# Where eighteen weight splits of a hybrid-block kernel run: GpSimd or VectorE

## The chip, the cores and the metric

The kernel runs on one NeuronCore of a Trainium2 chip. The metric is the device time of one execution in microseconds (us). The engines are named as in the profile: PE is TensorE (PEld its weight loads), DVE is VectorE, ACT is ScalarE, POOL is GpSimd, SP is SyncE.

## What is computed

The reference is one layer of a streaming encoder on a sequence of 1024 tokens of width 1024, in float32:

```python
def reference(...):
    x = x + token_mixer(rmsnorm(x, g_mix), w_in, gdn_conv, ..., w_sb_up, w_gdn_up, w_mix_out)
    x = x + memory_cross_attention(rmsnorm(x, g_cross), rmsnorm(mem, g_mem), w_cq, w_ckv, w_co)
    x = x + peer(rmsnorm(x, g_peer), w_pq, subkeys, peer_u, peer_v)
    return rmsnorm(x, g_final)
```

`token_mixer` makes one input projection. Of its columns, 1536 feed eight stick-breaking attention heads (`sb_q`, `sb_k`, `sb_v`), 1536 feed a gated DeltaNet through a causal convolution of width 4 (`g_q`, `g_k`, `g_v`), and the others are gates. `peer` scores 16384 single-neuron experts for every token by product keys, takes 8 x 16 of them, and sums `gelu(peer_u[e] . x) * gate * peer_v[e]` over them.

## The kernel before

The sequence is cut into three groups of 256, 384 and 384 tokens (GROUPS), and the loop at L1030 takes each through token mixing, cross attention and routing. The running state of the DeltaNet and the keys and values pass from group to group.

Every weight matrix goes through `proj` (L226). It takes 128 output columns at a time: SP loads the tile `raw` (128 x 1024), `split` (L85) makes two halves of it, and `mm3` (L219) multiplies. A split is two instructions: ACT copies `raw` into `wh` in the shorter type F32R (L77), and then `wl = raw - wh` is one `tensor_tensor` (L89), on VectorE or, where `split` is given `eng=pool`, on GpSimd. `mm3` issues three matmuls for every one of 8 row blocks: `wh` with the input's high part, `wl` with the high part, `wh` with its low part. There are three buffers of `raw` and two each of `wh` and `wl`.

Which engine makes `wl` is set by the argument `share`: with `share` at n, every n-th column tile has it on GpSimd. Four constants give it (L27): SH_G = 3 for the 12 tiles of the DeltaNet columns (L468), SH_S = 6 for the 12 tiles of the attention columns (L523), SH_R and SH_Z = 0 for routing (L688) and gates (L548), which is none. The other calls of `proj` pass no share. That makes 4 + 2 splits on GpSimd in each group, 18 in all. What follows a DeltaNet tile is a convolution: one ACT copy and three VectorE instructions (`gc`, L474 to L476, recorded at L77 and L83).

Three of the eight blocks of 128 tokens (DENSE = 4, 5, 6) are taken through all experts by dense products. `dense_h` (L932) splits a tile of `peer_u` and multiplies it, `weigh` (L959) splits a tile of `peer_v` and adds into six PSUM tiles. The first 36 tiles of `peer_u` are done ahead of the rest, in `dense_ahead` (L942), where one in four has its `wl` on GpSimd (L948).

The other five blocks gather the chosen rows. `fetch` (L791) issues an indirect DMA of 128 rows (512 KB) from GpSimd's queue into one of seven `row` buffers. Rows of `peer_u` are multiplied with the tokens and summed by one VectorE instruction (L809); rows of `peer_v` are added up on TensorE (L838) or, for blocks 3 and 7, on VectorE (L856, recorded at L83). The gathers of blocks 0 and 1 can begin when group 0 is routed, and run beside groups 1 and 2.

The program is traced in the order of the code and then ordered for each engine by a scheduler that works with its own estimates of durations (`schedule_with_timeline_sim=True`, L1133). The order of each engine's queue is fixed before the kernel starts: an instruction that waits holds all behind it on its engine.

Of the kernel before, what the change touches and what calls it, by code (L numbers as in the profile page):

```python
# [23 lines left out]
NMEM = 256  # L24
GROUPS = ((0, 256), (256, 384), (640, 384))
RG = 4
SH_G, SH_R, SH_S, SH_Z = 3, 0, 6, 0  # L27
DENSE = (4, 5, 6)
AHEAD = 36
FIRST = 320  # L30
SPOT = 1
LATER = 1
SUMMED = (3, 7)
ROWS = 7
# [17 lines left out]
def block_kernel(ctx: ExitStack, tc: tile.TileContext, x_t, mem_t, gains, cst, sel, eye, w_in, conv, a_log,  # L52
# [3 lines left out]
    act, vec, pe, pool, sp = nc.scalar, nc.vector, nc.tensor, nc.gpsimd, nc.sync  # L56

    def open_pool(name, bufs=1, space=None, side=None, where=ctx):
        kw = {}
        if space is not None:  # L60
            kw["space"] = space
        if side is not None:
            kw["side"] = side
        return where.enter_context(tc.tile_pool(name=name, bufs=bufs, **kw))
# [14 lines left out]
    def func(o, i, f, **kw):  # L79
        return act.activation(o, i, f, **kw)  # L80
# [4 lines left out]
    def split(hi, lo, src, scale=1.0, eng=vec):  # L85

        copy(hi, src, scale)
        if scale == 1.0:
            eng.tensor_tensor(lo, src, hi, op=OP.subtract)  # L89
        else:  # L90
            stt(lo, src, scale, hi, OP.mult, OP.subtract)
# [20 lines left out]
    def j_tile():  # L112
        return pp.tile([P, 512], F32, name="pj")
# [4 lines left out]
    def mix(a, b, ratio):  # L118

        n = 0.0  # L120
        for _ in b:
            n += ratio
            while n >= 1.0:
                next(a, None)
                n -= 1.0
        for _ in a:
            pass
# [9 lines left out]
    def run(*its):  # L137
        for _ in steps(*its):
            pass
# [79 lines left out]
    def mm3(ps, wh, wl, hi, lo, kt):  # L219
        i = 0  # L220
        for k in range(kt):
            for a, b in ((wh, hi), (wl, hi), (wh, lo)):
                pe.matmul(ps, lhsT=a[:, k], rhs=b[:, k], start=i == 0, stop=i == 3 * kt - 1)  # L223
                i += 1
# [692 lines left out]
    def pick_stored(tmp):  # L917
        for i, blk in enumerate(order):
            if i >= nlast:
                sel3 = tmp.tile([P, 3, P], F32, name="sel3")  # L920
                sp.dma_start(sel3, sel_sc[blk])
                yield from spread(tmp, sel3, i)

    def pick_gates(p2, found, tmp):
        for b in range(nlast):
            sel3 = choose_t(p2, *found(b))
            yield
            yield from spread(tmp, sel3, b)
# [3 lines left out]
    def dense_h(r, xh, xl, ps, o, eng=vec):  # L932

        raw = wp.tile([P, KD, P], F32, name="raw", bufs=3)
        sp.dma_start(raw, ut_v[:, :, r * P:(r + 1) * P])
        uh = wp.tile([P, KD, P], F32R, name="wh")
        ul = wp.tile([P, KD, P], F32R, name="wl", bufs=WLS)
        split(uh, ul, raw, eng=eng)
        mm3(ps, uh, ul, xh, xl, KD)
        func(o, ps, AF.Gelu)  # L940

    def dense_ahead(xh, xl, where):  # L942
        T = ND
        tmp = open_pool("dh", 2, where=where)
        for r0 in range(0, AHEAD, RG):
            h = tmp.tile([P, RG, T], F32, name="h")
            for j in range(RG):
                dense_h(r0 + j, xh, xl, j_tile()[:, :T], h[:, j], pool if j == 3 else vec)  # L948
                yield
            sp.dma_start(h_sc[:, r0:r0 + RG, :T], h)  # L950

# [54 lines left out]
    def retrieve(*blocks):  # L1006
        pending = None
        for blk in blocks:
            keep = []
            its = [retrieve_u(blk, keep)]  # L1010
            if pending:
                its.append(second(*pending))
            yield from steps(*its)
            pending = (blk, keep)
        yield from steps(second(*pending))
# [14 lines left out]
    for g, (t0, T) in enumerate(GROUPS):  # L1030
# [11 lines left out]
        with ex:  # L1042
            if last:
                picked = open_pool("picked", 1, side="right", where=ex)
            cross(g, x1[0], T)
            if last and SPOT == 0:
                run(pick_stored(picked))
# [6 lines left out]
        if g == 1:  # L1054
            run(retrieve(0, 1))
    if SPOT == 1:
        run(pick_stored(picked))
    if not LATER:
        for b in range(nlast, len(late)):
# [6 lines left out]
    with ExitStack() as eh:  # L1066
        mix(pick_gates(pool_c, found, picked), dense_ahead(xh, xl, eh), (nlast * 33) / max(AHEAD, 1))
    if LATER:
        for b in range(nlast, len(late)):
# [67 lines left out]
```

## Time and profile before

| | us |
|---|---|
| median of 3 runs | 3774.82 |
| lowest and highest | 3766.2, 3779.0 |
| the profiled execution, whole | 3750.96 |
| its span, first to last instruction | 3749.2 |
| PE busy in the span | 3356.5 |
| DVE busy | 2831.5 |
| POOL busy | 1848.1 |
| ACT busy | 1646.3 |

The profile is of one execution, and the sums below are made against its 3750.96 us; the median of the runs is 0.6% longer. Busy time of an engine holds the time in which an instruction is stretched by something else. Matmul ends are modelled, so a PE that is busy all the time need not be at its peak; the granted clock (PEclk) tells at which speed it was let run, 1.00 for 2.4 GHz and 0.50 for 1.2 GHz. In the stretches of the span, group 0 reaches to about 560 us, group 1 begins its projections at about 560, group 2 at about 1460, and the dense stage of the experts begins at about 2310, with `weigh` from 2812 on.

### The profile page before, as it was taken

The numbers are of one execution on the slowest core, as the hardware profiler recorded it, in microseconds if no ns is written. First come the engines' busy times: TensorE is split into PE (matmuls) and PEld (weight loads), VectorE is DVE, ScalarE is ACT, GpSimd is POOL, SyncE is SP. The second block draws the span as 40 slices with busy tenths as digits, with TensorE's granted clock in tenths as the row PEclk, the third lists the DMA queues.
The fourth block names the chain that finished last, engine by engine and source line by source line (L and its number), as shares of the span: only waits on it lengthen the run. The fifth ranks groups of instructions, "written<-read, shape, count | busy, mean of one in ns | idle before, by whom it ended". The sixth has DMA issues, their size and how long they took to land. (4 is left out here: it accounts for less than half of the span.)

```text
span 3749.2 us, 56321 instructions
## 1 busy us (share of the span) xinstructions
PE 3356.5 (90%) x20621; PEld 2821.2 (75%) x20621; DVE 2831.5 (76%) x5255; ACT 1646.3 (44%) x3086; POOL 1848.1 (49%) x1419
## 2 busy tenths in 40 slices
PE   7999976899879986999978899999759999999995
PEld 6888866777767774767757677888748999999974
DVE  5445599887566699427896666999887888879886
ACT  5754544654324333545523243367643333333333
POOL 1020006767754555456787545564663555536541
PEclk9999988999989997999969999999979999999998
DMA  5526548997899998999877999999999999989995
GB/s 155 146 85 197 155 127 286 325 314 257 285 361 332 339 343 291 320 312 316 287 251 246 368 302 333 325 338 329 358 366 338 330 340 341 346 294 365 350 381 205
DMA packets 745789, 1100.50 MB, mean 294 GB/s; under 512 B 42148, under 2 KB 554532, under 8 KB 742440
## 3 DMA queue, kind: packets, MB, share of 16 engines
q0 software_dynamic: 184320, 671.17, 49.5%
q1 hardware_dynamic: 561192, 425.73, 36.9%
q8 instruction: 162, 2.65, 0.3%
q14 instruction: 115, 0.94, 0.1%
HBM read 1036.60 MB, written 60.16 MB: 293 GB/s over the span
## 5 line engine op out<-in xcount | busy, mean ns | idle before, releaser
L793 POOL DMA_INDIRECT row<-in_peer_u_dram,ix x640 | 839.0, 1311 | 546.3 <-DVE hh L809 151.6
L809 DVE CUSTOM_DVE_ANT_0 row<-row,xs 128x1024 f32<-128x1024 f32 x640 | 837.9, 1318 | 124.7 <-DMA row<-in_peer_u_dram,ix 110.5
L89 DVE TENSOR_TENSOR wl<-raw,wh 128x1024 fp32r<-128x1024 f32 (+1 forms) x420 | 494.9, 1178 | 278.1 <-ACT wh L77 270.9
L223 PE MATMUL pj<-xhi,wh 128*128 128x384 f32 (+1 forms) x1912 | 640.6, 335 | 56.0 <-ACT xhi L77 21.1
L223 PE MATMUL pj<-xhi,wl 128*128 128x384 f32 (+1 forms) x1912 | 642.3, 336 | 36.6 <-POOL wl L89 24.0
L223 PE MATMUL pj<-xlo,wh 128*128 128x384 f32 (+1 forms) x1912 | 623.5, 329 | 6.2 <-DVE xlo L89 6.2
L793 POOL DMA_INDIRECT row<-in_peer_v_dram,it x384 | 435.6, 1134 | 368.4 <-PE ac L838 163.3
L77 ACT ACTIVATE wh<-raw 128x1024 fp32r<-128x1024 f32 (+1 forms) x447 | 449.9, 1007 | 277.5 <-PE pj L223 193.9
L793 POOL DMA_INDIRECT row<-in_peer_v_dram,ix x256 | 363.3, 1419 | 379.1 <-DVE y L83 200.2
L223 PEld LDWEIGHTS pj<-xhi,wh 128*128 128x128 f32 x1912 | 374.9, 196 | 88.8 <-ACT xhi L77 26.0
L223 PEld LDWEIGHTS pj<-xhi,wl 128*128 128x128 f32 x1912 | 375.3, 196 | 75.4 <-POOL wl L89 26.4
L223 PE MATMUL pj<-xh,wh 128*128 128x384 f32 x1152 | 393.9, 342 | 16.2 <-ACT h L80 12.9
L223 PE MATMUL pj<-xh,wl 128*128 128x384 f32 x1152 | 395.8, 344 | 9.9 <-DVE wl L89 7.5
L223 PE MATMUL pj<-xl,wh 128*128 128x384 f32 x1152 | 391.5, 340 | 0.2 <-DVE xl L89 0.2
L223 PEld LDWEIGHTS pj<-xlo,wh 128*128 128x128 f32 x1912 | 373.3, 196 | 23.6 <-DVE xlo L89 10.1
L83 DVE SCALAR_TENSOR_TENSOR y<-row,hh,y 128x1024 f32<-128x1024 f32 x256 | 330.3, 1290 | 6.0 <-DMA row<-in_peer_v_dram,ix 5.1
L838 PE MATMUL ac<-row,sb 128*32 128x256 f32 x3072 | 264.1, 401 | 37.6 <-DMA row<-in_peer_v_dram,it 35.7
L89 POOL TENSOR_TENSOR wl<-raw,wh 128x1024 fp32r<-128x1024 f32 x27 | 67.0, 2483 | 465.0 <-ACT wh L77 463.6
L223 PEld LDWEIGHTS pj<-xh,wh 128*128 128x128 f32 x1152 | 219.5, 191 | 26.0 <-ACT h L80 13.9
L223 PEld LDWEIGHTS pj<-xh,wl 128*128 128x128 f32 x1152 | 219.4, 190 | 24.2 <-DVE wl L89 9.0
L77 ACT ACTIVATE vh<-vr 128x1024 fp32r<-128x1024 f32 x128 | 135.0, 1058 | 202.5 <-PE pj L974 202.5
L223 PEld LDWEIGHTS pj<-xl,wh 128*128 128x128 f32 x1152 | 219.2, 190 | 1.5 <-DVE xl L89 0.6
(450 smaller groups left out, 6255.2 us busy)
## 6 DMA issues: line engine op xcount, KB each, us to landing
raw<-in_w_in_dram SPq DMA_DIRECT2D x132, 512.0 KB
raw<-in_peer_ut_dram SPq DMA_DIRECT2D x128, 512.0 KB
vr<-in_peer_v_dram SPq DMA_DIRECT2D x128, 512.0 KB
raw<-in_w_pq_dram SPq DMA_DIRECT2D x48, 512.0 KB
g_sc<-st SPq DMA_DIRECT2D x12, 2048.0 KB
gm<-g_sc SPq DMA_DIRECT2D x32, 768.0 KB
raw<-in_w_mix_dram SPq DMA_DIRECT2D x24, 512.0 KB
raw<-in_w_cq_dram SPq DMA_DIRECT2D x24, 512.0 KB
```

The costliest lines, as they stand in the source:

```text
L77: return act.activation(o, i, AF.Copy, scale=scale)
L83: return vec.scalar_tensor_tensor(out=o, in0=a, scalar=s, in1=b, op0=op0, op1=op1)
L89: eng.tensor_tensor(lo, src, hi, op=OP.subtract)
L223: pe.matmul(ps, lhsT=a[:, k], rhs=b[:, k], start=i == 0, stop=i == 3 * kt - 1)
L793: pool.indirect_dma_start(out=t, out_offset=None, in_=src, in_offset=bass.IndirectOffsetOnAxis(ap=index, axis=0))
L809: vec.tensor_tensor_reduce(out=t, in0=t, in1=xs, scale=1.0, scalar=0.0, op0=OP.mult, op1=OP.add, accum_out=hh[:, j:j + 1])
L838: pe.matmul(ac[32 * d:32 * d + 32, 256 * w:256 * w + 256], lhsT=sb[:, j], rhs=t[:, 256 * d:256 * d + 256], start=j == 0, stop=j == 31)
```

## The change

Two constants go to 0, so that `proj` gives no split of the DeltaNet and attention columns to GpSimd any more. The literal 3 in `dense_ahead` becomes a constant of the same value.

```diff
@@ -24,11 +24,12 @@
-SH_G, SH_R, SH_S, SH_Z = 3, 0, 6, 0
+SH_G, SH_R, SH_S, SH_Z = 0, 0, 0, 0
 DENSE = (4, 5, 6)
 AHEAD = 36
 FIRST = 320
 SPOT = 1
+PJ = 3
 LATER = 1
@@ -945,7 +946,7 @@
             for j in range(RG):
-                dense_h(r0 + j, xh, xl, j_tile()[:, :T], h[:, j], pool if j == 3 else vec)
+                dense_h(r0 + j, xh, xl, j_tile()[:, :T], h[:, j], pool if j == PJ else vec)
                 yield
```

## Rows read from the trace of the kernel before

**Rows 1.** The page: busy us by engine; POOL splits with count, busy, mean ns, idle.
```profile
PE 3356.5 (90%) x20621; PEld 2821.2 (75%) x20621; DVE 2831.5 (76%) x5255; ACT 1646.3 (44%) x3086; POOL 1848.1 (49%) x1419
...
L89 POOL TENSOR_TENSOR wl<-raw,wh 128x1024 fp32r<-128x1024 f32 x27 | 67.0, 2483 | 465.0 <-ACT wh L77 463.6
```
**Rows 2.** PE's waits over the span: us in total, times, longest.
```profile
PE ac L838 <- DMA row<-in_peer_v_dram,it: 35.7, 23, 5.1
...
PE pj L223 <- POOL wl L89: 26.3, 10, 10.2
```
**Rows 3.** PE's waits for POOL from 0 to 130, 560 to 750, 1460 to 1650 us.
```profile
PE pj L223 <- POOL wl L89: 2.6, 3, 1.0
...
PE pj L223 <- POOL wl L89: 16.3, 2, 10.2
...
PE pj L223 <- POOL wl L89: 5.2, 1, 5.2
```
**Rows 4.** Timeline, POOL beside DVE: start, us, engine, line, operation, idle before.
```profile
33.17 2.35 POOL L89 TENSOR_TENSOR wl<-raw,wh 128x1024 fp32r<-128x1024 f32 x1 [31.72 <-ACT wh L77]
34.07 2.54 DVE L89 TENSOR_TENSOR wl<-raw,wh 128x1024 fp32r<-128x1024 f32 x1 [4.13 <-ACT wh L77]
...
1525.78 2.38 POOL L89 TENSOR_TENSOR wl<-raw,wh 128x1024 fp32r<-128x1024 f32 x1
1525.97 2.62 DVE L83 SCALAR_TENSOR_TENSOR gc<-ev,cv,gc 128x384 f32<-128x384 f32 x1 [2.56 <-ACT gc L77]
```
**Rows 5.** Durations on DVE over the span: ns shortest, median, longest; first and last start.
```profile
L89 DVE TENSOR_TENSOR wl<-raw,wh x420: 682/1224/3359, 19.1 to 3536.3; 128x1024 fp32r<-128x1024 f32 x124, 128x512 fp32r<-128x512 f32 x16
...
L83 DVE SCALAR_TENSOR_TENSOR gc<-ev,cv,gc x108: 364/610/3391, 36.5 to 1538.6; 128x384 f32<-128x384 f32 x72, 128x256 f32<-128x256 f32 x36
```
**Rows 6.** Timeline in groups 1 and 2: ACT's `wh` and the splits.
```profile
566.19 1.05 ACT L77 ACTIVATE wh<-raw 128x1024 fp32r<-128x1024 f32 x1
570.02 1.22 DVE L89 TENSOR_TENSOR wl<-raw,wh 128x1024 fp32r<-128x1024 f32 x1
580.22 1.05 ACT L77 ACTIVATE wh<-raw 128x1024 fp32r<-128x1024 f32 x1
583.99 1.06 ACT L77 ACTIVATE wh<-raw 128x1024 fp32r<-128x1024 f32 x1 [2.12 <-PE pj L223]
587.62 2.52 POOL L89 TENSOR_TENSOR wl<-raw,wh 128x1024 fp32r<-128x1024 f32 x1
593.96 1.22 DVE L89 TENSOR_TENSOR wl<-raw,wh 128x1024 fp32r<-128x1024 f32 x1
663.51 1.04 ACT L77 ACTIVATE wh<-raw 128x1024 fp32r<-128x1024 f32 x1
667.49 1.21 DVE L89 TENSOR_TENSOR wl<-raw,wh 128x1024 fp32r<-128x1024 f32 x1
672.13 1.04 ACT L77 ACTIVATE wh<-raw 128x1024 fp32r<-128x1024 f32 x1
682.96 2.53 POOL L89 TENSOR_TENSOR wl<-raw,wh 128x1024 fp32r<-128x1024 f32 x1
1463.57 1.05 ACT L77 ACTIVATE wh<-raw 128x1024 fp32r<-128x1024 f32 x1
1465.74 1.22 DVE L89 TENSOR_TENSOR wl<-raw,wh 128x1024 fp32r<-128x1024 f32 x1
1471.17 2.35 POOL L89 TENSOR_TENSOR wl<-raw,wh 128x1024 fp32r<-128x1024 f32 x1
```
**Rows 7.** Windows: stretch, us, busy and count by engine, PEclk, DMA share, GB/s.
```profile
577.00:625.00 48.00, 32.83 (x162) 30.99 (x160) 44.15 (x67) 14.69 (x31) 35.44 (x26) 0.89 0.93 306
...
686.00:690.00 4.00, 4.00 (x14) 4.00 (x14) 4.00 (x8) 0.52 (x1) 3.39 (x3) 0.50 0.90 240
691.00:701.00 10.00, 10.00 (x58) 9.73 (x57) 6.69 (x9) 7.40 (x15) 4.49 (x5) 1.00 1.05 383
...
2830.00:3720.00 890.00, 877.76 (x4345) 785.15 (x4343) 735.81 (x855) 320.04 (x440) 434.39 (x299) 1.00 0.97 335
```

## The prediction

> **What bounds the kernel now.** I read the page first: TensorE (PE) is busy for 3356.5 of 3749.2 us and GpSimd (POOL) for half, and 27 weight splits on POOL take 67.0 us, 2483 ns each [rows 1]. So POOL is not short of time; what counts is who waits for it. The table of waits says that PE idled 26.3 us just in front of matmuls whose `wl` came from POOL, out of some 393 us of idle (3749.2 less 3356.5), and 35.7 us for fetched rows of `peer_v` [rows 2]. Asked by stretch, 2.6 us of the 26.3 lie in the projections of group 0, 16.3 in those of group 1 (two waits, the longer 10.2) and 5.2 in those of group 2, one wait [rows 3]. That is 24.1 us; the remaining 2.2 belong to the splits of L948, which the diff does not touch.
>
> Next I laid the timeline of POOL beside that of VectorE (DVE), and there is a second cost. When a POOL split starts, the two-input DVE instruction that meets it ends only after it: a split of 1.22 us takes 2.54 beside POOL's at 33.17, and a convolution step takes 2.62 beside the one at 1525.78 [rows 4]; the medians of the split and of the convolution step are 1.224 and 0.610 us [rows 5]. The rows given are the first and the last of 16 such meetings among the 18 splits that move; I subtracted the median of the same line, tile and shape from each, which gives 1.27 to 2.78 us each and 31.7 us together.
>
> Last the end of the kernel: from 2830 to 3720 PE is busy 877.76 of 890 us at full clock, with the DMA share at 0.97 [rows 7]. That stage is PE's own work, so an earlier start of it is an earlier end, as long as the row gathers keep up.
>
> **The change part by part.** SH_G and SH_S at 0 move 12 + 6 splits (of every 12 tiles, every third, and every sixth, in three groups) to DVE. PJ = 3 says what the literal said: the 9 splits of L948 stay on POOL.
>
> *DVE's queue.* Added are 18 x 1.224 = 22.0 us [rows 5], gone are the 31.7 us of holding: net 9.7 us less. In group 1, whose DVE is nearly full (44.15 of 48 us busy from 577 to 625 [rows 7]), six meetings cost 13.1 us against 7.3 added: 5.7 us less. I count nothing for this in the forecast and the 5.7 as a possible gain. A rule of the Trainium skill speaks against the change here: "Perfetto Trace Analysis", Optimizing Scalar/DVE Operations, says that where DVE is saturated, moving work to ScalarE or even GpSimd may help; by that alone DVE would be 22.0 us fuller and nothing would come back. The same passage warns that the port the two engines share can spoil such a move, and the 31.7 us of holding in this trace are what it warns of.
>
> *PE's waits, group 0.* ScalarE finishes `wh`, POOL needs about 2.4 us, PE takes `wl` at once. On DVE, mostly idle at those moments, the split is done 1.2 us sooner; the three waits are of at most 1.0 [rows 3]. All 2.6 us go.
>
> *Group 1.* The split at 587.62 had its `wh` at 581.27 (580.22 + 1.05), so it lay 6.35 us in POOL's queue behind fetches, and ended 8.87 after its `wh`; the one at 682.96 had its `wh` at 673.17, lay 9.79 and ended 12.32 after it [rows 6]. How long would DVE keep it? Twelve DVE splits between 566 and 672 show delays of 0.03 to 8.91 us, mean 3.44: the first waits 2.77 (from 567.25 to 570.02), the worst 8.91 (585.05 to 593.96), the last 2.94 [rows 6]. With 3.44 + 1.22 = 4.66 the savings are 8.87 - 4.66 = 4.2 and 12.32 - 4.66 = 7.7: 11.9 of the 16.3 us. The other four splits had no wait behind them worth naming. What is next late is DVE itself, with its row reductions.
>
> *Group 2.* `wh` was there at 1464.62, POOL's split began 6.55 later and ended at 1473.52; DVE did a split at 1465.74 and was free for another at 1466.96 [rows 6]. That ends at 1468.2, before PE has stalled: all 5.2 us go.
>
> *The granted clock.* After the waits PE runs at half speed for a while: from 686 to 690 it is granted 0.50 (1.2 GHz), with 14 matmuls in 4 us, against 58 in 10 us at 1.00 (2.4 GHz) right behind [rows 7]. 14 matmuls at 5.8 per us are 2.4 us of work, so 1.6 us were lost. Three such stretches, about 4.6 us. The waits of group 1 only shrink, so I count the 1.6 of group 2 alone.
>
> *POOL.* It gets 18 x 2.4 = 43 us back, and the fetches behind each split can be issued earlier. Whether one lands earlier depends on free row buffers and the DMA queues: between a loss of nothing and a gain that the rows do not show. I take 0.
>
> Sum: 2.6 + 11.9 + 5.2 + 1.6 = 21.3 us. Of this 18.7 arise in groups 1 and 2, beside the gathers, whose rows come at their own pace. Bounds: none of the 18.7 carries to the end if the gathers set it, all of it if PE does. Being 18.7 us earlier, PE would leave about six more rows to the last stage (POOL's 299 instructions there are fetches, 34 per 100 us); at 0.52 MB each (128 rows of 4 KB) and 335 GB/s [rows 7] that is 10 us of transfer in a stage of 0.97 share, of which some fits. The stage looks like PE's, so I keep three quarters: 2.6 + 14.0 = 16.6 us. The profiled execution took 3750.96 us (span 3749.2, 1.8 around it), 0.6% under the median of the runs, 3774.82. 3750.96 - 16.6 = 3734.4 is a ratio of 0.9956; on the median that is **3758 us**.
>
> **The rivals.**
> 1. *The gathers hold the end.* Only group 0's 2.6 us remain, since the gathers start after it: 3772 us. For: DMA share 0.97 in the last stage, waits for rows [rows 2, 7]. Against: PE hardly waits in that stage.
> 2. *DVE's queue becomes the wait* (slower). The moved splits stand in group 1 behind row reductions that wait for DMA. If all six are served like the worst of the twelve, they end 6 x (8.91 + 1.22) = 60.8 us after their `wh` in sum, against 34.7 now (delays 0.08, 6.35, 2.08, 1.58, 9.79, 0.13 and the splits' own times): 26.1 later, less 9.4 from groups 0 and 2: 16.7 us slower, 3792. It decides from a mean delay of 4.57 us on (POOL's mean 3.34 plus the 1.23 that DVE is quicker). For: DVE is 92% busy there. Against: the mean of its delays is 3.44, and holding goes. The Trainium skill's rule above, without its warning, would end in this rival.
> 3. *More than forecast.* All waits of POOL go (24.1), with the clock (4.6) and DVE's relief (5.7): 34.4 us, 3740.
> 4. *The change doesn't do what it says.* The title speaks of none on GpSimd, while nine splits stay there; they concern 2.2 us of waits, so the time does not hang on it.
>
> Over all lies that the order of every engine's queue is made anew from estimated durations (L1133), so that instructions far from the splits may change places. In the trace a single bad place costs PE 5 to 10 us (5.1 longest for rows, 10.2 for a POOL split [rows 2, 3]); two of them either way are 16 to 20.
>
> **How the numbers follow.** 0.3%, about what a measurement can tell here, is 11 us. Forecast (3758) 0.38, of which 0.04 ends within 0.3%; more (3740) 0.12; gathers (3772) 0.22; DVE's queue (3792) 0.28. Faster 0.34 + 0.12 = 0.46, same 0.04 + 0.22 = 0.26, slower 0.28. The range takes in 3740 and 3792 and a misplacement of 16 to 20 us beyond each: 3720 to 3808. The likeliest case alone spans 3740 to 3772.
>
> **What would show it.** POOL keeps nine instructions of L89 and DVE has 438 of that tile; no PE wait is put down to POOL `wl` before 2400; convolution steps and row reductions beside the old places are back at their medians (those beside the splits of L948 stay long); PE's waits on DVE `wl` grow by less than 24 us. The first two waits in group 1 are down to a few us, and the last stage starts some 15 us earlier. The forecast is wrong if PE's waits on DVE `wl` in 560 to 750 pass 16 us, if the stage from 2830 is longer by what was gained, or if large waits stand at lines that hold no split.

## The result, and the profile after

The changed kernel takes 3754.66 us (median of 13 runs, 3744.07 to 3765.22), the kernel before 3774.82 (13 runs). The ratio is 0.9945, 95% interval 0.9934 to 0.9955: 20 us less, where 3758 was forecast. Put on a chip again, it gave 0.9961 (0.9944 to 0.9977).

The forecast time was close; the place was not. The profile of before that the prediction rests on is of an execution 24 us under its median, so totals of the two first profiles can't be set against each other; a second profile of the kernel before (3773.59 us, below) is used where places are compared. In the changed kernel all lines behind L31 have numbers one higher.

The page of the changed kernel, busy us by engine:
```profile
PE 3363.0 (89%) x20621; PEld 2831.3 (75%) x20621; DVE 2820.2 (75%) x5273; ACT 1650.5 (44%) x3089; POOL 1840.4 (49%) x1401
...
L90 DVE TENSOR_TENSOR wl<-raw,wh 128x1024 fp32r<-128x1024 f32 (+1 forms) x438 | 513.1, 1172 | 260.6 <-ACT wh L78 246.4
```
Eighteen instructions have gone from POOL to DVE, and yet DVE is busy 11 us less than in [rows 1]. The durations on DVE say why (ns shortest, median, longest; first and last start):
```profile
L84 DVE SCALAR_TENSOR_TENSOR gc<-ev,cv,gc x108: 364/605/682, 34.8 to 1539.5; 128x384 f32<-128x384 f32 x72, 128x256 f32<-128x256 f32 x36
```
The longest convolution step was 3.391 us in [rows 5] and is 0.682 now. The timeline of VectorE in group 0, where a tile is 256 columns wide. The kernel before (first profile) has six convolution steps of 4.86 us in sum beside the POOL split at 47.27, and three of 3.32 beside the one at 58.57:
```profile
46.66 4.86 DVE L83 SCALAR_TENSOR_TENSOR gc<-ev,cv,gc 128x256 f32<-128x256 f32 x6
...
58.96 3.32 DVE L83 SCALAR_TENSOR_TENSOR gc<-ev,cv,gc 128x256 f32<-128x256 f32 x3 [0.91 <-ACT gc L77]
```
The changed kernel, in its second run, whose file keeps the old line numbers:
```profile
48.05 1.23 DVE L89 TENSOR_TENSOR wl<-raw,wh 128x1024 fp32r<-128x1024 f32 x1 [0.16 <-ACT wh L77]
49.19 1.52 DVE L83 SCALAR_TENSOR_TENSOR gc<-ev,cv,gc 128x256 f32<-128x256 f32 x3
50.88 1.23 DVE L89 TENSOR_TENSOR wl<-raw,wh 128x1024 fp32r<-128x1024 f32 x1 [0.17 <-ACT wh L77]
52.02 1.52 DVE L83 SCALAR_TENSOR_TENSOR gc<-ev,cv,gc 128x256 f32<-128x256 f32 x3
53.72 1.22 DVE L89 TENSOR_TENSOR wl<-raw,wh 128x1024 fp32r<-128x1024 f32 x1 [0.18 <-ACT wh L77]
```
A tile comes every 2.83 us, one split and three convolution steps, with hardly a gap. The 19 us from 45 to 64 by window (us, then busy time and count of PE, PEld, DVE, ACT and POOL, then granted clock, DMA share and GB/s); first the kernel before, from its first profile:
```profile
45.00:64.00 19.00, 15.63 (x122) 14.75 (x123) 15.84 (x20) 10.66 (x28) 5.04 (x2) 1.00 0.50 139
```
and the changed kernel, from its own first:
```profile
45.00:64.00 19.00, 19.00 (x163) 19.00 (x162) 17.60 (x29) 12.78 (x35) 0.00 (x0) 1.00 0.69 167
```
PE ran 163 matmuls instead of 122, at the same granted clock.

To see where a lead is made and lost, I read off each trace when ACT begins the `wh` copy of certain weight tiles (the weight tiles are loaded in one order in all kernels), and when the first fetch starts. First column in us, the others as differences from it:

| | before, second profile | before, first profile | changed, second run | changed, first run | group 0 alone | group 1 alone | group 2 alone | shifted in 1 and 2 | group 0 and shifted |
|---|---|---|---|---|---|---|---|---|---|
| last DeltaNet tile, group 0 | 68.0 | -0.8 | -9.9 | -9.7 | -9.0 | -0.5 | -2.2 | +0.1 | -9.8 |
| last attention tile, group 0 | 110.5 | -0.7 | -13.6 | -13.3 | -12.7 | -0.2 | -2.0 | +0.3 | -13.4 |
| first fetch | 578.6 | -1.8 | -15.8 | -18.8 | -20.0 | -1.4 | -6.1 | -0.4 | -19.6 |
| last attention tile, group 1 | 714.5 | -2.3 | -5.8 | -15.1 | -25.0 | +5.5 | -6.6 | -7.6 | -23.9 |
| first tile, group 2 | 1390.4 | -10.3 | -4.5 | -1.3 | -24.0 | +16.3 | -7.0 | -8.7 | -32.1 |
| last attention tile, group 2 | 1631.4 | -13.7 | -19.3 | -18.5 | -26.0 | +13.2 | -20.0 | -22.7 | -33.6 |
| first dense tile | 2421.1 | -17.5 | -18.0 | -19.3 | -30.2 | +9.7 | -8.8 | -11.4 | -14.6 |
| 37th dense tile | 2704.3 | -21.6 | -15.5 | -15.0 | -27.5 | +1.6 | +2.6 | -11.9 | +6.4 |
| end of the span | 3771.8 | -22.6 | -13.0 | -11.8 | -17.4 | +23.5 | +3.0 | -4.7 | +18.8 |

Each column is one execution. Up to the first fetch the two executions of one kernel lie at most 3.0 us apart; behind it the two of the kernel before drift 10.3 us apart by the first tile of group 2 and 22.6 by the end, with no change of program. A difference behind the first fetch, of one column, is therefore not shown to be the kernel's own unless it is clearly larger.

The lead of the changed kernel is there before the first gather starts. In both of its runs little of it is left at the first tile of group 2, and it is 18 to 19 us at the first dense tile, against the second profile; against the first profile of the kernel before it would be 0.5 to 1.8 there. Only the medians of the runs tell what reaches the end.

### The profile page after: what moved, and what is told of

It is laid out like the page before. It is cut to its first block, busy times and chain, and to the rows that moved or that the text cites. A ratio compares the mean times of both kernels' runs of the same rounds, so it can differ in the third digit from the quotient of the medians.

```text
span 3760.0 us, 56279 instructions
## 1 busy us (share of the span) xinstructions
PE 3363.0 (89%) x20621; PEld 2831.3 (75%) x20621; DVE 2820.2 (75%) x5273; ACT 1650.5 (44%) x3089; POOL 1840.4 (49%) x1401
## 5 line engine op out<-in xcount | busy, mean ns | idle before, releaser
L794 POOL DMA_INDIRECT row<-in_peer_u_dram,ix x640 | 861.3, 1346 | 927.9 <-DMA ix<-id_sc 346.0
L810 DVE CUSTOM_DVE_ANT_0 row<-row,xs 128x1024 f32<-128x1024 f32 x640 | 826.6, 1300 | 130.6 <-DMA row<-in_peer_u_dram,ix 110.4
L90 DVE TENSOR_TENSOR wl<-raw,wh 128x1024 fp32r<-128x1024 f32 (+1 forms) x438 | 513.1, 1172 | 260.6 <-ACT wh L78 246.4
L794 POOL DMA_INDIRECT row<-in_peer_v_dram,ix x256 | 372.3, 1454 | 352.9 <-DVE y L84 171.3
L224 PE MATMUL pj<-xh,wh 128*128 128x384 f32 x1152 | 396.0, 344 | 16.4 <-ACT h L81 13.2
L224 PEld LDWEIGHTS pj<-xh,wh 128*128 128x128 f32 x1152 | 220.4, 191 | 28.3 <-ACT h L81 14.6
L81 ACT ACTIVATE h<-pj 128x384 f32<-128x384 f32 x128 | 62.8, 490 | 327.5 <-PE pj L224 309.5
```

Of the source, the lines that this page charges most:

```text
L794: pool.indirect_dma_start(out=t, out_offset=None, in_=src, in_offset=bass.IndirectOffsetOnAxis(ap=index, axis=0))
L810: vec.tensor_tensor_reduce(out=t, in0=t, in1=xs, scale=1.0, scalar=0.0, op0=OP.mult, op1=OP.add, accum_out=hh[:, j:j + 1])
```

## The experiments

**The kernel before and the changed kernel again, and the change in halves.** The halves make the share depend on the group:
```diff
-            for i, ps in proj(w_in, O_G, 1536, xh, xl, T, share=SH_G):
+            for i, ps in proj(w_in, O_G, 1536, xh, xl, T, share=SH_G if g in (1, 2) else 0):
-                for i, ps in proj(w_in, O_SB, 1536, xh, xl, T, share=SH_S):
+                for i, ps in proj(w_in, O_SB, 1536, xh, xl, T, share=SH_S if g in (1, 2) else 0):
```
for group 0 alone, and `g in (0,)` for groups 1 and 2.

> The kernel before once more, for a second profile: the first one was of an execution 24 us under the median. Up to the first gather (576.8 us) all theories expect the same times within 1 us, behind it differences of up to 20 us with no change of program.

> The changed kernel once more, on the same chip as the two halves. All theories: ratio 0.9934 to 0.9955. If the two halves add, their differences sum to this one. Its profile tells which stretches keep the lead of 16 to 17 us that the first profile shows at the first gather.

> The splits of group 0 alone move to VectorE (6 of the 18); groups 1 and 2 keep theirs on GpSimd. Theory A (the gain is made in group 0, where the splits on GpSimd also hold VectorE's own instructions and so delay every following tile, and it carries to the end): 16 to 20 us less than the kernel before, ratio about 0.995, first gather some 16 us earlier than 576.8. Theory B (the prediction's own sum: most of the gain lies in groups 1 and 2): 2.6 us less, ratio 0.9993. Theory C (the gain comes from queues laid out anew far from the splits): nothing fixed; a first gather that is earlier, with a total that is not.

> The splits of groups 1 and 2 move (12 of 18), those of group 0 stay on GpSimd. Theory A: no change, ratio within 0.998 to 1.002, since in group 1 VectorE's queue keeps a split as long as GpSimd's did. Theory B: 14 us less (three quarters of 18.7), ratio 0.9963. Theory C: nothing fixed.

Measured: group 0 alone 3756.24 us, ratio 0.9962 (0.9950 to 0.9974), 17 us less; groups 1 and 2 together 3779.4, ratio 1.0017 (1.0004 to 1.0030), 6 us more. On the same chip the whole change gave 0.9961, 15 us less. So the six splits of group 0 give as much as the whole, and the twelve of groups 1 and 2 nothing that reaches the end: theory A, against my own sum. The second profile of the kernel before started its first gather at 578.6 us (576.8 in the first), and ended 22.6 us later than the first: what lies behind the first gather differs that much between executions of one program.

**Holding without a late result.** The changed kernel, with four GpSimd subtractions in group 0 whose result `junk` nobody reads (the operands are shortened, and the line that makes the tile `junk` is left out):
```diff
                 for j in range(1, 4):
                     stt(d, c[:, j:j + T], cv[:, i, j:j + 1], d, OP.mult, OP.add)
+                if g == 0 and i % 3 == 2:
+                    pool.tensor_tensor(junk, cs[:, 0:8]..., d[:, None, :].to_broadcast([P, 4, T]), op=OP.subtract)
```


> The changed kernel (no projection split on GpSimd) with four extra GpSimd subtractions of two SBUF inputs, 128x1024 float32, in group 0, one after the convolution of each third DeltaNet tile. Nothing reads their result, so TensorE never waits for them, and VectorE's queue is the same up to 64 us. If holding of VectorE costs time by itself (theory A), each stretches a VectorE instruction by 1 to 2 us and the last DeltaNet split of group 0 comes 4 to 8 us later than in the changed kernel. If only the late arrival of the split's result costs time, it comes at the same time within 0.5 us.

Timeline of POOL in this kernel:
```profile
42.87 3.37 POOL L479 TENSOR_TENSOR junk<-cs,gc 128x1024 f32<-128x1024 f32 x1 [41.41 <-DVE gc L83]
52.84 2.40 POOL L479 TENSOR_TENSOR junk<-cs,gc 128x1024 f32<-128x1024 f32 x1 [6.60 <-issue]
```
and of DVE:
```profile
42.74 1.23 DVE L89 TENSOR_TENSOR wl<-raw,wh 128x1024 fp32r<-128x1024 f32 x1
43.88 3.69 DVE L83 SCALAR_TENSOR_TENSOR gc<-ev,cv,gc 128x256 f32<-128x256 f32 x3
47.48 1.22 DVE L89 TENSOR_TENSOR wl<-raw,wh 128x1024 fp32r<-128x1024 f32 x1
48.62 1.52 DVE L83 SCALAR_TENSOR_TENSOR gc<-ev,cv,gc 128x256 f32<-128x256 f32 x3
50.05 1.22 DVE L89 TENSOR_TENSOR wl<-raw,wh 128x1024 fp32r<-128x1024 f32 x1
51.19 1.52 DVE L83 SCALAR_TENSOR_TENSOR gc<-ev,cv,gc 128x256 f32<-128x256 f32 x3
53.04 3.29 DVE L89 TENSOR_TENSOR wl<-raw,wh 128x1024 fp32r<-128x1024 f32 x1 [0.33 <-ACT wh L77]
```
Three convolution steps take 3.69 us beside the first idle subtraction instead of 1.52, a split 3.29 beside the second instead of 1.22; the four hold VectorE for 7.4 us in sum. Up to 130 us PE, ACT and VectorE have the same instructions in the same order as in the changed kernel (second run), so the subtractions are the only difference. The last DeltaNet tile comes 4.2 us later than there, with two of the four done by then, and the last attention tile, behind all four, 7.4 us later; 0.6 us of both was there before the first subtraction. PE's waits from 0 to 130 us in this kernel (us in total, times, longest):
```profile
PE pj L223 <- DVE wl L89: 6.9, 4, 1.9
```
against 0.6 us in the changed kernel's second run. Holding alone costs PE's path about 1.7 us for each GpSimd instruction (6.8 over four), and PE's waits show it under VectorE's name. The whole kernel took 3780.09 us in its one timed run, longer than the kernel before: in the terms of the table it is 12.8 us early at the first fetch and 6.5 late at the end.

**Groups 1 and 2 one by one, and an order that moves nothing.** `g in (0, 2)` and `g in (0, 1)` in the edit above; and all 18 splits on GpSimd, but in groups 1 and 2 those of the tile before:
```diff
-            split(..., eng=pool if share and c // P % share == share - 1 else vec)
+            split(..., eng=pool if share and (c // P + at) % share == share - 1 else vec)
```
with `at = int(g > 0)`.

> The six splits of group 1 alone move to VectorE. Prediction's sum: 11.9 us of TensorE's waits less, 9 us in the end, ratio 0.9976. Rival of VectorE's queue: up to 26 us more, ratio up to 1.007. From the run with groups 1 and 2 moved (1.0017): 1.000 to 1.003, with 18 us of waits on GpSimd gone and about as much come back as waits on VectorE and ScalarE.

> The six splits of group 2 alone move. Prediction's sum: 5.2 + 1.6 us less of TensorE's time, 5 in the end, ratio 0.9987. If the gathers or the new order of the queues decide there: 0.998 to 1.004, without a link to the 5.2 us wait, which goes in any case.

> All 18 splits stay on GpSimd; in groups 1 and 2 they are those of the tiles one place earlier (of each three, the second; of each six, the fifth). No work is added or removed, so this shows what another order of the queues alone is worth there. If the order matters little: ratio 0.999 to 1.001 and GpSimd waits of 15 to 25 us. If theory C holds: up to 0.4% either way, as much as the moves of groups 1 and 2 gave.

Measured: group 1 alone 1.0044 (1.0029 to 1.0059), group 2 alone 1.0034 (1.0019 to 1.0049), shifted 0.9974 (0.9964 to 0.9985). The two single moves would add to 0.78% and are 0.17% together; the shift, which changes no work, gains 9 us (3762.35 against 3771.52). PE's waits from 535 to 760 us, in the second profile of the kernel before:
```profile
PE pj L223 <- POOL wl L89: 18.2, 2, 11.5
PE pj L223 <- ACT ev L77: 14.6, 4, 8.5
...
PE pj L223 <- ACT wh L77: 5.3, 3, 2.5
...
PE pj L223 <- DVE wl L89: 0.9, 2, 0.5
```
with group 1 alone moved:
```profile
PE pj L223 <- ACT ev L77: 23.2, 7, 5.3
PE pj L223 <- ACT wh L77: 15.6, 6, 5.3
PE pj L223 <- DVE wl L89: 10.7, 6, 6.1
```
and shifted:
```profile
PE pj L223 <- ACT ev L77: 17.2, 3, 10.9
PE pj L223 <- ACT wh L77: 7.5, 5, 2.9
...
PE pj L223 <- POOL wl L89: 6.1, 2, 4.4
```
Moving the splits turns 18.2 us of waits on POOL into 28.7 more on ACT and DVE: these four lines go from 39.0 to 49.5. Shifting them takes 12 us off POOL's line without any split leaving it: the two long waits hang on the places that the splits have in POOL's queue, and are not the price of every split on POOL. Group 2 alone is another case: from the first to the last attention tile of group 2 it gains 13 us (table, -7.0 to -20.0), and it has lost all of that by the 37th dense tile, where no split was moved. But the shifted kernel, whose splits there are all on POOL, gains 14 in the same stretch (-8.7 to -22.7), so the 13 us are not shown to come from moving the splits.

**Without gathers.** `run(retrieve(0, 1))` and the rest of `retrieve` left out, so that five of the eight blocks get no expert output, in both kernels:
```diff
         if g == 1:
-            run(retrieve(0, 1))
+            pass
...
-    rest = retrieve(*fetched[2:])
-    for _ in range(FIRST):
-        next(rest)
-    mix(rest, dense(xh, xl), ...)
+    mix(iter(()), dense(xh, xl), ...)
```


> The kernel before without its row gathers and all that uses them (five of eight blocks get no expert output): the reference for the next run. All theories: much shorter than the whole kernel, the splits of groups 1 and 2 beside an idle GpSimd and a VectorE that has no row reductions.

> The changed kernel without its row gathers, the same work left out. If a split on GpSimd costs about 2 us wherever the queues run freely, and it was the gathers that swallowed the gain of groups 1 and 2: 30 to 40 us less than the kernel before without gathers. If those splits cost nothing in groups 1 and 2 by themselves: 13 to 17 us less, group 0's part alone. If the new order decides: anything between, with the lead lost at places that hold no split.

Measured: 3224.88 and 3200.08 us, 0.8562 and 0.8488 of the kernel before; 25 us apart in the medians, 19.8 in the two profiles. The lead in those profiles is 12.8 us at the last attention tile of group 0, 17.7 at the first tile of group 1, 20.8 at the last attention tile of group 1, 25.8 at that of group 2, and 18 to 20 from the first dense tile on. So without gathers the lead grows by 3.1 us over the six splits of group 1 and by 7.3 over those of group 2 (20.8 less 17.7; 25.8 less the 18.5 at the first tile of group 2), 0.5 and 1.2 us a split against some 2 us in group 0, and 7 us are lost again by the first dense tile. I expected 30 to 40 if the gathers alone had swallowed them; that is refuted. That the twelve are worth something there by themselves is not shown: the lead also grew by 4.9 us (12.8 to 17.7) between the projections of group 0 and those of group 1, where no split was moved.

**Two gains together, and the title in full.** Group 0 on VectorE with the shift; and all 27 splits on VectorE, the nine of L948 too.

> Group 0's splits on VectorE, those of groups 1 and 2 on GpSimd one tile earlier: the two changes that gained, together. If they add: 0.9962 x 0.9974, ratio 0.9936. If the order of the queues is a lottery behind group 0: anything from 0.992 to 1.000, with the first gather still 14 to 19 us earlier.

> What the title says in full: the nine splits of the dense stage on VectorE too. They hold VectorE for 16.8 us in sum in the profile of before and cost TensorE 2.2 us of waits. If the dense stage ahead is bound there by VectorE: up to 10 us less than the changed kernel, ratio to the kernel before 0.993. If they do not matter: the changed kernel's 0.994 to 0.996.

Measured: group 0 and shifted 1.0057 (1.0041 to 1.0073), the slowest of all, although each part alone gains. Its first fetch is 19.6 us early and its last attention tile of group 2 33.6, and all is lost between there and the 37th dense tile (table). All 27 on VectorE: 3746.63 us, ratio 0.9935 (0.9917 to 0.9953), the fastest kernel here, 0.6% under the kernel before. Its interval overlaps that of the change, and its order is a new one too, so I don't credit the 8 us between them to the nine splits.

## Why the prediction was right, and where not

*The time.* 3758 forecast, 3754.66 measured. The sum behind it was 2.6 us from group 0 and 14.0 from groups 1 and 2. The runs show 17 us less from group 0 alone and 6 more from groups 1 and 2. The two mistakes nearly cancel, so that the forecast came within 4 us is luck.

*Group 0, the mis-sized term.* 2.6 us forecast, 12.7 to 13.6 measured at the last attention tile (0.3 to 1.1 of it from before POOL's first split), 16 to 20 at the first fetch. The step that failed is "I count nothing for this in the forecast", said of the holding. I had found it, summed it (31.7 us) and set it against DVE's busy time, and took from PE's waits only those put down to POOL [rows 3]. But an instruction of DVE that is held passes its lateness on under DVE's name. In the window from 0 to 130 the kernel before has beside 2.6 us on POOL also these (first profile):
```profile
PE pj L223 <- DVE wl L89: 5.7, 6, 2.2
...
PE pj L223 <- ACT wh L77: 3.2, 3, 1.7
```
and the changed kernel has
```profile
PE pj L224 <- ACT wh L78: 2.2, 2, 1.7
...
PE pj L224 <- DVE wl L90: 0.5, 1, 0.5
```
11.5 us became 2.7. With the granted clock, 0.80 before and 0.90 after from 28 to 45 us (another 1.7 us of work, an estimate from these two levels), 10.5 of about 12 us are accounted for.

The first profiles show where the 12 us arise. When POOL's first split starts the changed kernel is 0.6 us ahead, at the last attention tile 12.6 (`wh` at 97.26 instead of 109.86). Of this 5.1 come between the fourth and the fifth `wh` (32.98 and 44.44 before, 32.38 and 38.73 after). Holding is 1.3 us there: the split of [rows 4] at 34.07 takes 2.54, and PE waits 2.2 for it, the longest of the six. The rest is order: before, PE does the matmuls of the two waiting tiles by turns, and ACT's copy of the first result, which stands ahead of the next `wh`, begins after 45 of the two tiles' 48 matmuls:
```profile
44.07 0.38 ACT L77 ACTIVATE ev<-pj 128x256 f32<-128x256 f32 x1 [5.18 <-PE pj L223]
```
In the changed kernel it begins at 38.35, after 27. Beside the four POOL splits from 47 to 91 us VectorE is held for 7.6 us in sum, and the lead grows by 6.9, about as much per us of holding as with the idle subtractions (7.4 held, 6.8 late, without a single wait on POOL). So somewhat more than half of group 0's lead goes with holding. How the 5.1 us divide between the later result, the new order and what holding adds to them was not separated.

*Group 1.* Right that the waits on POOL would go, and that DVE's queue would keep a split; wrong in how long. Before, PE waited 6.07 us for the split at 587.62 of [rows 6]:
```profile
590.19 0.69 PE L223 MATMUL pj<-xhi,wl 128*128 128x384 f32 x1 [6.07 <-POOL wl L89]
```
The split that stands for it in the changed kernel:
```profile
560.35 1.05 ACT L78 ACTIVATE wh<-raw 128x1024 fp32r<-128x1024 f32 x1
...
567.28 1.23 DVE L810 CUSTOM_DVE_ANT_0 row<-row,xs 128x1024 f32<-128x1024 f32 x1 [5.85 <-DMA row<-in_peer_u_dram,ix]
...
570.33 1.21 DVE L90 TENSOR_TENSOR wl<-raw,wh 128x1024 fp32r<-128x1024 f32 x1
...
571.60 0.69 PE L224 MATMUL pj<-xhi,wl 128*128 128x384 f32 x1 [6.42 <-DVE wl L90]
```
`wh` was ready at 561.40 and the split began 8.93 us later, behind a row reduction that had waited 5.85 us for its row: the mechanism of the second rival, at the worst value that [rows 6] had shown. PE waited 6.42 us where 6.07 were to shrink. The split that stands for the one at 682.96 was 5.27 us late; PE's wait fell from 10.2 to 2.06. Over the six the mean delay is 3.98 us (0.09, 8.93, 4.28, 5.26, 5.27, 0.04), between the 3.44 that I took and the 4.57 at which the rival decides, so a split is done 0.6 us earlier than on POOL. The waits on ACT beside it grew instead (`ev` from 15.9 to 20.7 us, 560 to 750). DVE has no room left there; from 577 to 625 it is busy 47.84 of 48 us, after 44.15 before [rows 7]:
```profile
577.00:625.00 48.00, 30.51 (x134) 28.93 (x133) 47.84 (x83) 12.56 (x26) 36.39 (x25) 0.82 0.96 316
```

*Group 2.* The 5.2 us wait went as forecast: no wait on POOL is left before 2400. That this gains time was not shown: the lead within the projections (-7.0 to -20.0 with group 2 alone) comes with the shift as well, and it does not carry to the end.

*What carries.* Group 0's lead carried whole in its own run and without gathers. But the order of the queues, which I had put at 16 to 20 us either way, is worth as much as the change itself: 9 us less for a shift that changes no work, 24 more (3792.38 against 3768.77) for that shift with group 0's gain in it. So the lead before the gathers is shown, while how much of it reaches the end in one given kernel depends on an order that I can't derive; the measured 20 us hold for this one. Which instruction loses the lead in the kernels that lost it was not found.

*The rest.* POOL keeps nine splits and DVE has 438, as said. Waits on DVE `wl` over the span fell from 25.7 to 22.9 us instead of growing. The last stage is PE's as before (883.51 of 890 us busy from 2830 to 3720), and `weigh` begins 18 us earlier than in the second profile of the kernel before, where 15 were forecast, for the wrong reason (4.6 us later than in the first). One of the prediction's signs of being wrong did appear, a larger wait at a line that holds no split, PE's for the gates' product `gr`, before and after:
```profile
PE pj L223 <- DVE gr L598: 12.7, 8, 3.4
...
PE pj L224 <- DVE gr L599: 16.6, 8, 8.5
```

## What to carry to other kernels

A helper engine that reads SBUF can cost more through what it holds up than through what waits for its result: look for instructions of the neighbour engine that are longer than their median exactly beside the helper's, and put the waits for those on the helper's account. Read each stage by itself; in this kernel the same move gave 2 us per split in group 0, where a tile has 2.8 us of matmuls and little else to do, and nothing that reached the end in groups 1 and 2, where VectorE also has the row reductions. Where a scheduler lays the queues out anew with every edit, run an edit that changes no work to learn what the order alone is worth before crediting a gain below half a per cent.

## What the runs showed of the hardware

A GpSimd subtraction of two SBUF inputs, 128x1024, takes about 2.4 us against 1.22 on VectorE, and a two-input VectorE instruction that meets it does not end until after it (16 of the 18 splits of the kernel before, 1.27 to 2.78 us each). It goes the other way too: the idle subtraction at 42.87 started inside a VectorE split that ended at 43.97 and took 3.37 us instead of 2.40. Which of the two is held can't be read from the start times alone: in three of the 16 the VectorE instruction had started first, by 0.18 to 0.56 us, and was held all the same, as the row reduction that takes 3.88 us from 603.46 beside this split:
```profile
603.84 2.42 POOL L89 TENSOR_TENSOR wl<-raw,wh 128x1024 fp32r<-128x1024 f32 x1
```
The Trainium skill ("SBUF — State Buffer", Who interferes with whom) says that a VectorE instruction with two SBUF inputs contends with a GpSimd instruction that reads SBUF, and calls the port pair that they share an exclusive lock. The traces agree that the two contend, in both directions, and the longest convolution step falling from 3.391 to 0.682 us is its size here.
